# Hybrid retention and sliding-window layer: every SBUF place and PSUM bank named by the plan that orders the kernel

## The chip, the cores and the metric

The kernel runs on one core of one Trainium2 chip. The metric is the time of one execution in device microseconds (us); less is better. Below, PE is TensorE, PEld its weight loads, DVE is VectorE, ACT is ScalarE, POOL is GpSimd, and SP is the engine whose queue issues nearly all DMAs.

## The reference

One pre-normalised mixer layer over 2048 tokens of width 1024, all float32:

```python
h = rms_norm(x, norm_w)
proj = einsum('bsd,de->bse', h, w_in)                 # 1024 -> 2816
rq, rk, rv, rg, sq, sk, sv, sg = split(proj)
ro = retention(rotary(rq), rotary(rk), rv)            # 4 heads, chunks of 128, recurrent state
ro = group_norm(ro) * ret_norm_w * silu(rg)
so = sliding_window_attention(sq, sk, sv, ...)        # 8 query heads, 2 key heads, window 128,
so = so * silu(sg)                                    # QK-norm, relative bias, a sink per head
x = x + einsum('bse,ed->bsd', concat([ro, so]), w_out)
```

## The kernel before

The sequence is cut into 16 chunks of 128 tokens, handled as 8 pairs. The three wide parts of the input projection and the output projection are done as seven block products m for each pair p (a Strassen-like scheme: sums and differences of quarters of the weights and of x, then seven products instead of eight). Each float32 operand is split into a high and a low part (`hi`, on ACT; `lo`, on DVE), and each product is three matmuls (`acc<-w,x`), which make up most of PE's work. Beside them run the window attention (`attend`, `values`: tiles `lg`, `pm`, `pT`, `own`, `so`), the retention (`keys_of`, `update`, `retain`, `group_norm`: tiles `qk`, `state`, `sT`, `ro`), and the gates (`gate`: tiles `g`, `go`).

Tiles are turned (transposed) in one of two ways. Some go through PE. The others go by DMA: `turn_by_dma` has ACT pull the two 16-bit halves of the floats apart into a tile `apart`, stores that to DRAM (`planes_dram<-apart`), and loads it back with a transposing DMA. Other stores to DRAM that matter here are `g_dram<-c` (a gate that waits for its stage) and `ro_dram<-ro` (the normalised retention).

No engine's order is written by hand. Each piece of work is an `Op` with a cost by engine, a due time, and the buffers that it reads and writes. `Program.emit` is a planner: it keeps a clock for each engine, takes the op that can start first, calls its function, and so writes the program op by op. Class `Order` chains all instructions in that order, so the tile framework below it can't move any of them; the framework adds the semaphore waits.

The planner also keeps places. There are 93 SBUF tiles of 128x512 (tag "k"), 8 of 128x256 ("h"), 8 PSUM banks ("bank"), and a few places for each small tile. `slots[tag]` is the sorted list of the times at which, by the plan, the free places come free: the end of the last op that used one, plus `SEM` (0.06 us). An op that needs a place takes the first time of the list. The plan counts a DMA as ended 2.6 us after its turn on the bus (`dma`: `(0.15 + kb / 450, 2.6, issue)`).

Which physical place a tile gets is not the planner's decision. `alloc` asks a pool for a tile with `bufs=CAP[b.tag]`, and the framework hands out one of the free ones. In the built program that is, for the 128x512 tiles, the place whose last user stands first in the program's order, or one of the two next to it, in 1492 of 1502 reuses. When the last user of a place was a store, the new tile's first writer waits until that store has landed.

All instructions are recorded through one helper, so the profile puts almost everything on line 390; the tiles' names tell groups apart.

Of the kernel before, what the change touches and what calls it, by code (L numbers as in the profile page):

```python
# [29 lines left out]
F32 = mybir.dt.float32  # L30
# [9 lines left out]
P = 128  # L40
# [16 lines left out]
CAP = {"k": 93, "h": 8, "bank": 8}  # L57
SMALL, COUNTS = 3, {"ms": 1, "rxt": 1, "rqk0t": 1, "rqk1t": 1}
# [23 lines left out]
SEM = 0.06  # L82
# [19 lines left out]
def change(a, b):  # L102

    return 0.0 if a == b else LESSER if 0 < a < 3 and 0 < b < 3 else CHANGE
# [3 lines left out]
class Buf:  # L108


    def __init__(self, tag=None, shape=None, dtype=F32, name="", share=None, ap=None):
        self.tag, self.shape, self.dtype, self.name, self.share = tag, shape, dtype, name, share
        self.ap, self.left, self.end = ap, 0, 0.0
        self.writer, self.readers = None, []

    def __call__(self):
# [18 lines left out]
class Program:  # L135
# [33 lines left out]
    def emit(self):  # L169
        engines = self.engines  # L170
        avail = {e: [] for e in engines}
        free = dict.fromkeys(engines, 0.0)
        port, table, bus, cut = 0.0, None, 0.0, 0
        cap = dict(CAP)
        slots = {t: [0.0] * n for t, n in cap.items()}
        used = dict.fromkeys(SHARE, 0)
        count = len(self.ops)

        def offer(o):
            for e in o.cost:  # L180
                bisect.insort(avail[e], (o.due, o.n, o))

        for o in self.ops:
            if not o.left:
                offer(o)
        done, now = 0, 0.0
        while done < count:
            best = None
            for e, found in avail.items():
                top = None  # L190
                base = free[e]
                if e == "T" and not cut:
                    crowd = sum(o.set in CUTS and o.ready <= base for _, _, o in found[:48])
                for due, n, o in found[:48]:
                    if top is not None and top[0] <= base + 1e-9 and not e == "T":
                        break
                    occ, lat, shared = o.cost[e]
                    s = max(base, o.ready)
                    if e == "T" and o.set:
                        if cut and o.set in CUTS:  # L200
                            s = max(base, o.ready + INSIDE)
                            if change(cut, CUTS[o.set]) < CHANGE:
                                due -= SOONER
                        else:
                            s = max(base, o.ready + SETTLED)
                            if o.set in CUTS:
                                due += LATER - CROWD * min(crowd, MOST)
                    if shared and e != "Q":
                        s = max(s, port)
                    need, short, room = {}, False, 0.0  # L210
                    for b in o.new:
                        if b.ap is None:
                            need.setdefault(b.tag, []).append(b)
                    if any(due > now + AHEAD_OF.get(b.share, 1e9) for b in o.new):
                        continue
                    spare = 0
                    if e == "Q" and need:
                        if due > now + AHEAD:
                            break
                        spare = SPARE  # L220
                    for tag, bs in need.items():
                        if tag not in slots:
                            slots[tag] = [0.0] * COUNTS.get(tag, SMALL)
                        f = slots[tag]
                        if len(f) < len(bs) + (spare if tag == "k" else 0):
                            short = True
                            break
                        room = max(room, f[len(bs) - 1])
                        for share in {b.share for b in bs if b.share}:
                            many = used[share] + sum(b.share == share for b in bs)  # L230
                            if many > SHARE[share] - (spare if share in SPARED else 0):
                                short = True
                    if short:
                        continue
                    s, wait = max(s, room), 0.0
                    if e == "A" and o.set and table and o.set != table:
                        wait = 1.3
                        s += 2.0
                    if top is None or s < top[0] - 1e-9 or (s < top[0] + 1e-9 and due < top[1]):
                        top = (s, due, n, o, wait, room)  # L240
                if top is not None and (best is None or top[:3] < best[0][:3]):
                    best = top, e
            if best is None:
                self.stuck(avail, used, slots)
            (s, _, _, o, wait, room), e = best
            occ, lat, shared = o.cost[e]
            free_before = free[e]
            for e2 in o.cost:
                a = avail[e2]
                a.pop(bisect.bisect_left(a, (o.due, o.n)))  # L250
            for b in o.new:
                if b.ap is None:
                    slots[b.tag].pop(0)
                    if b.share:
                        used[b.share] += 1
                    b.ap = self.alloc(b)
            if e == "Q":
                occ, lat, more = o.cost[e]
                bus = max(bus, s) + occ
                free[e] = max(s + more, bus - BACKLOG)  # L260
                o.end = bus + lat
            else:
                if wait:
                    s = s - 2.0 + wait
                if e == "A" and o.set:
                    table = o.set
                free[e] = s + occ
                o.end = s + lat
                if shared:
                    port = s + occ  # L270
                if e == "T":
                    s = max(free_before, o.ready, room) if o.set else s
                    s += change(cut, CUTS.get(o.set, 0))
                    cut = ENDS.get(o.set, CUTS.get(o.set, 0))
                    free[e] = s + occ
                    o.end = s + lat
            o.seen = free[e]
            if e == "T" and o.set is None:
                now = max(now, o.due)
            o.go(engines[e])  # L280
            done += 1
            if LOG is not None:
                LOG.append((e, s, free[e], o))
            for b in o.bufs:
                b.left -= 1
                b.end = max(b.end, o.end)
                if not b.left and b.tag:
                    bisect.insort(slots[b.tag], b.end + SEM)
                    if b.share:
                        used[b.share] -= 1  # L290
            for d in o.after:
                d.left -= 1
                same = len(d.cost) == 1 and e in d.cost and e in ("T", "A", "Q") and not o.label.startswith("load")
                t = o.seen if same and e != "Q" else o.end + SEM
                if e == "Q" and now > 0:
                    t += LATE
                if t > d.ready:
                    d.ready, d.by = t, o
                if not d.left:
                    offer(d)  # L300
        self.time = max(free.values())
# [92 lines left out]
def layer(ctx, tc, xt, xfirst, xtok, nw, w_in, w_rn, qkw, sinks, biasg, rope, decays, dmask, gpow, w_out, out):  # L394
# [5 lines left out]
    sbuf = ctx.enter_context(tc.tile_pool(name="pool", bufs=1))  # L400
    little = ctx.enter_context(tc.tile_pool(name="small", bufs=SMALL))
    psum = ctx.enter_context(tc.tile_pool(name="psum", bufs=1, space=PSUM))
    dram = ctx.enter_context(tc.tile_pool(name="dram", bufs=1, space=DRAM))

    def alloc(b):
        if b.tag == "bank":
            return psum.tile([P, 512], F32, tag=b.tag, bufs=CAP[b.tag], name=b.name)
        if b.tag in ("k", "h"):
            n = 512 if b.tag == "k" else 256
            return sbuf.tile([P, n], b.dtype, tag=b.tag, bufs=CAP[b.tag], name=b.name)  # L410
        return little.tile(b.shape, F32, tag=b.tag, bufs=COUNTS.get(b.tag, SMALL), name=b.name)

    prog = Program(alloc, {"V": V, "G": G, "A": A, "Q": Q, "T": T})
    op = prog.op

# [1261 lines left out]
```

## Time and profile before

| | us |
|---|---|
| runs | 710.24, 712.25, 712.52 (median 712.25) |
| the profiled execution: its own time | 713.38 |
| its span | 711.6 |
| PE busy | 687.2 (97%) |
| DVE busy | 605.7 (85%) |
| ACT busy | 474.1 (67%) |
| DMA queue of SP, share of 16 engines | 84.4% |

The span runs from the first to the last instruction of the program; the profiled execution's own time is 1.8 us longer. A PE that is busy 97% of the span is still not at its peak: matmuls are pipelined, and while the granted clock is halved each of them takes twice as long and still counts as busy. In the views of waits a row reads: who waited, for whom, us in total, how many times, the longest. In the timeline a row reads: start, duration, engine, instruction, count, and in brackets the idle time ahead of it and what ended it.

### The profile page before, as it was taken

Reading aid. Unit: us, or ns where it says so; the run is one execution under the profiler, and the core shown is the slowest. Engines: PE = TensorE matmul, PEld = TensorE weight load, DVE = VectorE, ACT = ScalarE, POOL = GpSimd, SP = SyncE. Lnnn points to the kernel's source line nnn. Section 1 sums busy time; section 2 is a strip of 40 time slices with the busy share of each in tenths; the row PEclk is TensorE's granted clock in tenths of the full one; section 3 lists DMA queues with packets and bytes.
Section 4 is the critical chain, followed back from the end, with each engine's and each line's share of the span. In section 5 each row is a group of like instructions: output and inputs, shape, how many; then the busy total and the mean of one; then the engine's idle time right before and its main releaser. Section 6 shows DMA issues by size and latency. Waiting matters only on the chain. (4 is left out here: it accounts for less than half of the span.)

```text
span 711.6 us, 15589 instructions
## 1 busy us (share of the span) xinstructions
PE 687.2 (97%) x5428; PEld 580.3 (82%) x5428; DVE 605.7 (85%) x1483; ACT 474.1 (67%) x1122; POOL 42.7 (6%) x75
## 2 busy tenths in 40 slices
PE   9999999999999999999899799999989999999998
PEld 7888888889899999987687578888768787788886
DVE  6999877877998979999797779899788698999962
ACT  7666955666796576989577668896989844253300
POOL 1000000025120010101000000100000000000000
PEclk9999999999999999999999989999999999999999
DMA  9999945989988899999999899589799898314722
GB/s 326 385 343 311 386 163 181 358 278 279 311 218 222 185 318 312 317 283 281 305 236 285 207 240 287 128 258 289 200 333 313 195 273 261 119 44 159 275 107 97
DMA packets 171487, 179.07 MB, mean 252 GB/s; under 512 B 71824, under 2 KB 106768, under 8 KB 171408
## 3 DMA queue, kind: packets, MB, share of 16 engines
q1 hardware_dynamic: 171264, 178.07, 84.4%
q8 instruction: 43, 0.70, 0.4%
q14 instruction: 36, 0.29, 0.1%
q10 hardware_dynamic: 144, 0.00, 0.0%
HBM read 106.64 MB, written 56.69 MB: 230 GB/s over the span
## 5 line engine op out<-in xcount | busy, mean ns | idle before, releaser
L390 PE MATMUL acc<-w,x 128*128 128x512 f32 (+1 forms) x2700 | 598.9, 380 | 8.2 <-ACT s L390 3.8
L390 PEld LDWEIGHTS acc<-w,x 128*128 128x128 f32 x2700 | 495.8, 190 | 95.1 <-ACT s L390 5.1
L390 DVE TENSOR_TENSOR x<-x 128x512 fp32r<-128x512 f32 (+2 forms) x220 | 146.4, 686 | 20.3 <-ACT x L390 19.9
L390 ACT ACTIVATE x<-x 128x512 fp32r<-128x512 f32 (+1 forms) x187 | 111.4, 616 | 18.6 <-DVE x L390 12.7
L390 DVE TENSOR_TENSOR w<-w 128x512 fp32r<-128x512 f32 (+3 forms) x96 | 61.0, 655 | 4.6 <-ACT w L390 2.2
L390 ACT ACTIVATE pm<-lg,nm 128x128 f32<-128x128 f32 x128 | 49.7, 395 | 6.7 <-DMA planes_dram<-apart 3.4
L390 ACT ACTIVATE w<-w 128x512 fp32r<-128x512 f32 (+1 forms) x72 | 40.4, 602 | 18.1 <-DVE w L390 11.3
L390 DVE SCALAR_TENSOR_TENSOR w<-w,nw_sb 128x512 fp32r<-128x512 f32 (+3 forms) x72 | 49.0, 703 | 0.8 <-ACT w L390 0.7
L390 DVE TENSOR_TENSOR s<-acc,s 128x512 f32<-128x512 f32 (+1 forms) x64 | 41.6, 651 | 8.0 <-PE acc L390 7.9
L390 DVE CUSTOM_DVE_ANT_0 lg<-m,bias,nsnk 128x160 f32<-128x160 f32 x128 | 42.5, 379 | 6.5 <-PE m L390 6.3
L390 POOL TENSOR_SCALAR_AFFINE_SELECT own<-pT 64x512 f32<-64x512 f32 x32 | 25.6, 813 | 266.2 <-ACT pT L390 218.8
L390 DVE TENSOR_TENSOR t<-acc,t 128x512 f32<-128x512 f32 (+2 forms) x33 | 21.2, 641 | 18.8 <-PE acc L390 18.2
L390 ACT ACTIVATE x<-go 128x512 fp32r<-128x512 f32 x40 | 24.0, 624 | 14.3 <-PE acc L390 7.4
L390 ACT ACTIVATE s<-acc 128x512 f32<-128x512 f32 (+1 forms) x32 | 18.0, 563 | 18.7 <-PE acc L390 10.1
L390 DVE TENSOR_TENSOR x<-go,x 128x512 fp32r<-128x512 f32 x40 | 27.1, 683 | 3.4 <-ACT x L390 3.4
L390 ACT ACTIVATE w<-w,nw_sb 128x512 fp32r<-128x512 f32 (+3 forms) x44 | 28.1, 680 | 2.3 <-DMA w<-in_w_in 2.3
L390 ACT ACTIVATE apart<-qn 128x1024 uint16<-128x1024 uint16 x16 | 16.9, 1055 | 16.2 <-DVE qn L390 16.1
L390 ACT ACTIVATE ro<-ro,nmu,rg 128x128 f32<-128x128 f32 x64 | 25.1, 481 | 3.3 <-DVE nmu L390 3.3
L390 ACT ACTIVATE c<-acc 128x512 f32<-128x512 f32 (+1 forms) x24 | 13.4, 559 | 19.2 <-PE acc L390 16.5
L390 ACT ACTIVATION_READ_ACCUMULATOR pm<-lg,nm 128x1 f32 x128 | 24.8, 194 | 0.0
L390 DVE TENSOR_TENSOR t<-acc,s 128x512 f32<-128x512 f32 (+1 forms) x32 | 20.7, 648 | 4.2 <-PE acc L390 4.1
L390 ACT ACTIVATE xk<-xk 128x512 f32<-128x512 f32 x32 | 19.8, 620 | 5.5 <-DMA xk<-in_xtok 5.5
(133 smaller groups left out, 666.8 us busy)
## 6 DMA issues: line engine op xcount, KB each, us to landing
x<-in_xt SPq DMA_DIRECT2D x80, 256.0 KB, 5.2
x<-s_dram SPq DMA_DIRECT2D x64, 256.0 KB, 4.6
planes_dram<-apart SPq DMA_DIRECT2D x56, 256.0 KB, 4.8
w<-in_w_in SPq DMA_DIRECT2D x40, 256.0 KB, 4.8
s_dram<-x SPq DMA_DIRECT2D x32, 256.0 KB, 4.5
xk<-in_xtok SPq DMA_DIRECT2D x32, 256.0 KB, 5.3
res<-in_xtok SPq DMA_DIRECT2D x32, 256.0 KB, 5.0
w<-in_w_out SPq DMA_DIRECT2D x20, 256.0 KB, 5.6
```

Source lines behind the costliest of these rows:

```text
L390: return lambda *a, **k: self.order.put(op(*a, **k))
```

## The change

The planner's list of free places now holds pairs: the time at which a place comes free by the plan, and the number of the place. A buffer remembers the number that it was given, and gives it back with its end. `alloc` makes the number part of the tag and asks for one buffer of that tag. So each named place is a pool of one, and a tile goes to the place that the plan took: the one that by the plan came free first.

```diff
-        slots = {t: [0.0] * n for t, n in cap.items()}
+        slots = {t: [(0.0, i) for i in range(n)] for t, n in cap.items()}
...
-                        room = max(room, f[len(bs) - 1])
+                        room = max(room, f[len(bs) - 1][0])
...
-                    slots[b.tag].pop(0)
+                    b.place = slots[b.tag].pop(0)[1]
...
-                    bisect.insort(slots[b.tag], b.end + SEM)
+                    bisect.insort(slots[b.tag], (b.end + SEM, b.place))
...
     def alloc(b):
+        tag = f"{b.tag}{b.place}"
         if b.tag == "bank":
-            return psum.tile([P, 512], F32, tag=b.tag, bufs=CAP[b.tag], name=b.name)
+            return psum.tile([P, 512], F32, tag=tag, bufs=1, name=b.name)
         if b.tag in ("k", "h"):
             n = 512 if b.tag == "k" else 256
-            return sbuf.tile([P, n], b.dtype, tag=b.tag, bufs=CAP[b.tag], name=b.name)
-        return little.tile(b.shape, F32, tag=b.tag, bufs=COUNTS.get(b.tag, SMALL), name=b.name)
+            return sbuf.tile([P, n], b.dtype, tag=tag, bufs=1, name=b.name)
+        return little.tile(b.shape, F32, tag=tag, bufs=1, name=b.name)
```

No instruction moves: on every engine the rows of the built program stand in the same order, and the numbers of places are the same (93, 8, 8). What changes is the address of a tile, and with it the earlier user for whose end its first writer waits. Four places follow. Names in brackets are semaphores: DMAHW0 to DMAHW7 are raised by landing DMAs, the others by the engine of that name.

ACT, where the retention's outputs `ro` of one pair of chunks are copied from PSUM; before:

```order
L390 ACTIVATE qk_5978<-qk_5978,factors1_83 128x64 [waits DVE_49,PE_49]
L390 ACTIVATE qk_5978<-qk_5978,factors1_83 128x64 x3
L390 ACTIVATE ro_6051<-m_5929 128x2x128 [waits DVE_49,PE_49]
L390 ACTIVATE ro_6051<-m_5931 128x2x128 [waits PE_49]
L390 ACTIVATE ro_6077<-m_5930 128x2x128 [waits DMAHW4_49,Activation_49]
L390 ACTIVATE ro_6077<-m_5932 128x2x128 [waits PE_49]
```

The same place in the changed kernel:

```order
L390 ACTIVATE qk_5978<-qk_5978,factors1_83 128x64 [waits DMAHW1_49]
L390 ACTIVATE qk_5978<-qk_5978,factors1_83 128x64 x3
L390 ACTIVATE ro_6051<-m_5929 128x2x128 [waits DVE_49,PE_49]
L390 ACTIVATE ro_6051<-m_5931 128x2x128 [waits PE_49]
L390 ACTIVATE ro_6077<-m_5930 128x2x128
L390 ACTIVATE ro_6077<-m_5932 128x2x128 [waits PE_49]
```

The first writer of `ro_6077` waited for the store out of `apart_5989`, whose place it took over; now it waits for nothing.

ACT, at softmax weights `pm`, a split `x`, and a copy `s` of a product's bank; before:

```order
L390 ACTIVATE ro_5198<-m_5056 128x2x128 [waits PE_49]
L390 ACTIVATE pm_5164,den_5162<-lg_5139,nm_5132 128x128 [waits DMAHW4_49,DVE_49]
L390 ACTIVATE pm_5164,den_5162<-lg_5139,nm_5132 128x128
L390 ACTIVATE x_5221<-x_4897 128x512 [waits DMAHW7_49,DMAHW2_49,Activation_49]
L390 ACTIVATE s_5228<-acc_5118 128x512 [waits PE_49]
```

The same place in the changed kernel:

```order
L390 ACTIVATE ro_5198<-m_5056 128x2x128 [waits PE_49]
L390 ACTIVATE pm_5164,den_5162<-lg_5139,nm_5132 128x128 [waits DMAHW0_49,DVE_49]
L390 ACTIVATE pm_5164,den_5162<-lg_5139,nm_5132 128x128
L390 ACTIVATE x_5221<-x_4897 128x512 [waits DMAHW2_49]
L390 ACTIVATE s_5228<-acc_5118 128x512 [waits DMAHW4_49,PE_49]
```

The store of `apart` for which `pm_5164` waited (DMAHW4) is now waited for by `s_5228`, three instructions later; `pm_5164` waits for an older transfer, and `x_5221` no longer for the store of another `apart` (DMAHW7).

ACT, at a copy `c` and two `apart` in front of a copy `s`; before:

```order
L390 ACTIVATE qk_5539<-qk_5539,factors1_83 128x64 x4
L390 ACTIVATE c_5627<-acc_5441 128x512 [waits DMAHW2_49,PE_49,Activation_49]
L390 ACTIVATE apart_5633<-qk_5539 128x1024 [waits Activation_49]
L390 ACTIVATE apart_5648<-qn_5544 128x1024 [waits DVE_49]
L390 ACTIVATE s_5661<-acc_5612 128x512 [waits PE_49]
```

The same place in the changed kernel:

```order
L390 ACTIVATE qk_5539<-qk_5539,factors1_83 128x64 x3
L390 ACTIVATE c_5627<-acc_5441 128x512 [waits DVE_49,PE_49]
L390 ACTIVATE apart_5633<-qk_5539 128x1024 [waits DMAHW0_49,Activation_49]
L390 ACTIVATE apart_5648<-qn_5544 128x1024 [waits DMAHW2_49]
L390 ACTIVATE s_5661<-acc_5612 128x512 [waits PE_49]
```

The wait for the store `g_dram<-c` (DMAHW2) went from `c_5627` to `apart_5648`, two instructions later, and `apart_5633` got one for an earlier store.

SP, at the loads of the residual `res` in the output projection, before and then in the changed kernel:

```order
L390 DMA res_8752<-in_xtok 128x512 [waits DMAHW6_49]
L390 DMA res_8754<-in_xtok 128x512 [waits PE_49]
L390 DMA res_8778<-in_xtok 128x512 [waits DMAHW0_49,DVE_49,Activation_49]
L390 DMA res_8803<-in_xtok 128x512 [waits DMAHW1_49,PE_49,Activation_49]
L390 DMA res_9035<-in_xtok 128x512 [waits DMAHW2_49,DVE_49]
```

```order
L390 DMA res_8752<-in_xtok 128x512 [waits DVE_49,Activation_49]
L390 DMA res_8754<-in_xtok 128x512 [waits DMAHW2_49]
L390 DMA res_8778<-in_xtok 128x512 [waits DMAHW0_49,DVE_49]
L390 DMA res_8803<-in_xtok 128x512 [waits DMAHW1_49,PE_49]
L390 DMA res_9035<-in_xtok 128x512 [waits DVE_49]
```

Each load waits for the end of another tile than before; `res_8778` and `res_8803` now wait for an instruction of DVE and one of PE that stand later in the program than the ones before.

More of the change, by code (lines that the diff above doesn't have):

```diff
@@ L112, in __init__ @@
         self.tag, self.shape, self.dtype, self.name, self.share = tag, shape, dtype, name, share
-        self.ap, self.left, self.end = ap, 0, 0.0
+        self.ap, self.left, self.end, self.place = ap, 0, 0.0, None
         self.writer, self.readers = None, []
@@ L222, in emit @@
                         if tag not in slots:
-                            slots[tag] = [0.0] * COUNTS.get(tag, SMALL)
+                            slots[tag] = [(0.0, i) for i in range(COUNTS.get(tag, SMALL))]
                         f = slots[tag]
```

## The prediction

> **What bounds the kernel now.** First the head of the page: the span, and the busy time of the engines.
>
> ```profile
> span 711.6 us, 15589 instructions
> ...
> PE 687.2 (97%) x5428; PEld 580.3 (82%) x5428; DVE 605.7 (85%) x1483; ACT 474.1 (67%) x1122; POOL 42.7 (6%) x75
> ```
>
> PE is idle for 711.6 - 687.2 = 24.4 us, so that is nearly all that a change of waits can give back, beside time in which PE runs at a lower clock. Next the view of waits for PE (who waits, for whom, us in total, times, longest):
>
> ```profile
> PE m L390 <- ACT ro L390: 6.2, 2, 4.3
> PE acc L390 <- ACT s L390: 3.8, 3, 2.0
> PE m L390 <- DVE sT L390: 3.5, 2, 2.9
> ...
> PE acc L390 <- DVE w L390: 1.4, 1, 1.4
> ```
>
> PE never waits long for DMA. It waits for ACT and DVE. So the question is what these wait for ahead of a PE stall; ACT's own waits hold two large ones that end with a store, not with data that ACT reads:
>
> ```profile
> ACT s L390 <- DMA planes_dram<-apart: 7.2, 1, 7.2
> ...
> ACT ro L390 <- DMA planes_dram<-apart: 5.0, 1, 5.0
> ```
>
> Neither `s` nor `ro` reads `planes_dram`. These are waits for a place: the tile before it in the same place was still being stored. The timeline around the longest PE stall shows it:
>
> ```profile
> 400.78 1.06 ACT L390 ACTIVATE apart<-qk 128x1024 uint16<-128x1024 uint16 x1 [1.04 <-DMA ro_dram<-ro]
> ...
> 404.67 1.36 PE L390 MATMUL m<-v,qk 64*64 64x128 f32 x32 [1.84 <-ACT ro L390]
> ...
> 405.01 0.36 SPq L390 DMA_DIRECT2D planes_dram<-apart  x1
> ...
> 409.92 0.66 ACT L390 ACTIVATE ro<-m 128x256 f32<-128x256 f32 x2 [5.04 <-DMA planes_dram<-apart]
> ...
> 410.36 0.48 PE L390 MATMUL m<-ident,kn 128*128 128x128 f32 x1 [4.33 <-ACT ro L390]
> ```
>
> SP issues the store at 405.01, it lands 4.8 us later, ACT may then overwrite the place, and PE, which needs the bank that ACT empties, starts at 410.36. The stall has a second price. Two pieces of the chain of waits (start, duration, count), and rows of windows (window, length, busy us of PE, PEld, DVE, ACT and POOL, granted clock, DMA share, GB/s):
>
> ```profile
> 410.84 5.96 PE acc L390 x15
> ...
> 432.44 9.75 PE acc L390 x42
> ```
>
> ```profile
> 340.00:420.00 80.00, 69.53 (x703) 54.56 (x702) 62.76 (x192) 54.55 (x141) 2.39 (x4) 0.91 0.97 262
> 400.00:420.00 20.00, 13.83 (x135) 10.62 (x135) 12.07 (x42) 12.03 (x33) 0.95 (x2) 0.74 0.91 249
> 520.00:540.00 20.00, 17.10 (x155) 13.56 (x154) 17.48 (x44) 18.40 (x32) 0.00 (x0) 0.91 1.13 331
> 351.30:354.70 3.40, 3.40 (x10) 2.63 (x9) 3.40 (x8) 1.11 (x3) 0.00 (x0) 0.50 1.03 298
> 375.00:385.00 10.00, 8.54 (x39) 6.67 (x38) 7.67 (x25) 7.65 (x15) 0.00 (x0) 1.00 1.00 263
> ```
>
> Undisturbed, a matmul takes 9.75 / 42 = 0.232 us; behind the stall it takes 5.96 / 15 = 0.397 us, and the granted clock of 400 to 420 is 0.74. That is 5.96 - 15 x 0.232 = 2.5 us lost on top of the idle time. Outside the few stretches where the clock falls there is nothing else to gain from it.
>
> The end is set by PE: its last long run begins at 621.37, and whatever brings that point forward brings the end forward.
>
> ```profile
> 621.37 87.04 PE acc L390 x394
> ```
>
> **The change part by part.** No instruction is added, removed or moved; only the earlier user of each place, and so the wait of its next first writer, is another. Below, each wait of the changed program is read against this trace: it would have ended when its releaser ended here.
>
> C, 404 to 416. `ro_6077` waits for nothing any more, so ACT can run it right behind the copy at 404.5, and the 4.33 us in front of PE's 410.36 go. The `apart` at 400.78 waits for older stores of `ro`, which had landed by 397, so its 1.04 us go. The row of DVE ahead of that burst lost time to a place as well, and ACT's normalising of `ro` waited for it:
>
> ```profile
> 390.42 0.43 DVE L390 TENSOR_TENSOR qk<-tcos,tsin 128x256 f32<-128x256 f32 x1 [1.82 <-DMA g_dram<-c]
> ...
> 390.96 1.27 ACT L390 ACTIVATE ro<-ro,nmu,rg 128x128 f32<-128x128 f32 x3 [2.47 <-DVE nmu L390]
> ```
>
> That wait goes too. 1.04 + 1.82 is more than the 1.84 us of the stall at 404.67, so both of PE's waits for `ro` go: 6.2 us, and the slow matmuls behind them, 2.5: together 8.7.
>
> A, 350. The timeline:
>
> ```profile
> 347.26 0.40 ACT L390 ACTIVATE pm<-lg,nm 128x128 f32<-128x128 f32 x1 [1.81 <-DMA planes_dram<-apart]
> ...
> 349.25 0.63 ACT L390 ACTIVATE x<-x 128x512 fp32r<-128x512 f32 x1 [1.11 <-DMA planes_dram<-apart]
> 349.79 0.58 ACT L390 ACTIVATE s<-acc 128x512 f32<-128x512 f32 x1
> ...
> 350.42 4.85 PE L390 MATMUL acc<-w,x 128*128 128x512 f32 x13 [2.01 <-ACT s L390]
> ```
>
> `pm` and `x` lose their waits; `s` inherits the store that ended `pm`'s, at about 347.2, and so ends near 347.8 instead of 350.4. PE's 2.0 us go. The window at 351.3 shows the clock at 0.50: 4.85 - 13 x 0.232 = 1.8 us more. Together 3.8.
>
> B, 380:
>
> ```profile
> 372.71 0.41 SPq L390 DMA_DIRECT2D g_dram<-c  x1
> ...
> 377.36 0.60 ACT L390 ACTIVATE c<-acc 128x512 f32<-128x512 f32 x1 [2.05 <-PE acc L390]
> ...
> 379.75 0.59 ACT L390 ACTIVATE s<-acc 128x512 f32<-128x512 f32 x1
> ...
> 380.39 3.02 PE L390 MATMUL acc<-w,x 128*128 128x512 f32 x12 [1.46 <-ACT s L390]
> ```
>
> The view names PE for `c`'s wait, but the product that it copies was complete at 373.5; the other semaphore in its wait is that of the store issued at 372.71, some 4.5 us before. In the changed program `c` goes 2 us earlier and the second `apart` behind it takes over that wait, so `s` comes about 1.4 us earlier: 1.4.
>
> D, 590 to 601:
>
> ```profile
> 590.88 0.60 ACT L390 ACTIVATE s<-acc 128x512 f32<-128x512 f32 x1 [7.19 <-DMA planes_dram<-apart]
> ...
> 592.84 0.69 DVE L390 TENSOR_TENSOR w<-w 128x512 fp32r<-128x512 f32 x1 [1.47 <-DMA planes_dram<-apart]
> ...
> 600.93 1.43 PE L390 MATMUL acc<-w,x 128*128 128x512 f32 x5 [1.36 <-DVE w L390]
> ```
>
> ACT's `s` could start 2.3 us earlier, with its product. DVE's `w` then waits for the end of ACT's split and of the DVE instruction ahead, 1.3 us earlier, and the packed DVE row behind it follows. PE's waits of 0.35 (the third for `s`: 3.8 - 2.0 - 1.46) and 1.36 shrink by about 1.6 in all.
>
> A to D: 3.8 + 1.4 + 8.7 + 1.6 = 15.5. The stall of 2.9 us for `sT` near 528 stays: no wait for a place stands in front of it.
>
> What is late next. A to C ask for 13.9 us out of the 80 from 340 to 420. DVE is busy 62.76 of them and ACT 54.55, so both fit into 66. The DMA engines hardly do: a share of 0.97 over 80 us is 77.6, and the highest share of any stretch of 20 us is the 1.13 at 520. At that rate the same transfers need 77.6 / 1.13 = 68.7 us, so DMA caps the gain there at 11.3. Loads are issued well ahead, so this is a soft cap; I take it, because the stores on which places hang are among those transfers.
>
> New waits. The latest releasers, against this trace, are two loads of `res` on SP (2.5 us late at 612.4; a later matmul must end first) and a split of `x` on ACT, the third of this row, that must now let the first `w` of DVE end (1.2 us late):
>
> ```profile
> 612.42 0.33 SPq L390 DMA_DIRECT2D res<-in_xtok  x1
> ...
> 615.42 1.68 ACT L390 ACTIVATE x<-x 128x512 fp32r<-128x512 f32 x3 [1.42 <-DVE x L390]
> ...
> 617.02 1.89 DVE L390 TENSOR_TENSOR w<-w 128x512 fp32r<-128x512 f32 x3
> ...
> 625.44 1.89 DVE L390 TENSOR_TENSOR x<-x 128x512 fp32r<-128x512 f32 x3
> ...
> 635.17 3.38 SPq L390 DMA_DIRECT2D res<-in_xtok  x3
> ```
>
> SP issues nothing behind that load until 635.17, and DVE uses the split only with the second of its three rows from 625.44 on, so both are covered here at no cost. PE itself gets no wait that would have been late in this trace. Once PE is ahead, covers are thinner: I bound the new waits by 0 and 2.5 + 1.2 = 3.7, and with no row nearer to either end take 1.9.
>
> Sum: 11.3 + 1.6 - 1.9 = 11.0. The profiled execution, 713.4 us with 1.8 outside its span, would come to 702.4; it ran 1.1 above the median of 712.25, from which the forecast is 701.3.
>
> A rule weighs against one term. The Trainium skill, in "TensorE: Matmul & The Clock Gate", section "Part 1: The HAM clock gate", says that an idle window of about 3.4 us is what halves PE's clock. By that rule the 2.0 us stall at 350 would not, and the forecast without its 1.8 us would be 703.1; the trace differs, with a clock of 0.50 from 351.3 on, while after the 1.46 us stall at 380 it stayed at 1.00. The row decides.
>
> **The rivals.** *Everything returns* (faster still): DMA is no cap, because loads run ahead. For it: shares above 1 at 351 and 520. Against it, the DMA row of the page (tenths in 40 slices of 17.8 us), which is at 8 or 9 nearly throughout from slice 10 to 23, up to 427:
>
> ```profile
> DMA  9999945989988899999999899589799898314722
> ```
>
> 15.5 off the median gives 696.8; with part of the `sT` stall and its slow clock gone as well, about 694.
>
> *Only the bare waits return.* PE comes to the next input that is not ready soon behind each stall removed. For it: PE's waits are short and many engines are near full. The 4.3 of C, less some of the new waits, remain: 712.25 - 4.3 = 708, between 705 and 710.
>
> *No effect.* The waits for stores move to neighbours that PE waits for as well, as A's did to `s`. Against it: there the store lands 2.6 us before `s` ran. About 712.
>
> *Slower.* The mechanism is the clock: with transfers pressed together, stores land later than the 4.8 us seen, a place wait stalls PE for 2 us or more around 430 to 450, where the changed program has its other late waits (up to 1.1 us on SP, 0.9 on ACT), and each such stall costs its length plus about 2 us of half clock. It decides only if these stalls sum to more than 15.5 + 2.1, two stalls like C's; with two the time is about 712.25 - 15.5 + 2 x 8.7 = 714, more with a third.
>
> **How the numbers follow.** A change under 0.3% (2.1 us) can't be told from none. Chances: the forecast (gain 8 to 14) 0.42; everything returns 0.20; bare waits 0.24; no effect 0.08; slower 0.06. So faster 0.86, same 0.08, slower 0.06. The range takes in the forecast, the bare waits up to 709.5 and everything returned down to 694.5: 0.8 or a little more.
>
> **What would show it.** In the changed profile ACT should have no wait of several us that ends with a store; PE's two waits for `ro` should be gone, and the granted clock near 1.00 from 400 to 420; the 2.9 us for `sT` should be there; the last run of PE should start near 610 and still last 87 us. I am wrong if PE shows new stalls of 2 us or more with a lower clock between 420 and 600, or if the stalls go and PE then waits for loads.

## The result, and the profile after

The changed kernel took 703.36 us (median of five runs, 699.02 to 706.88) against 712.25 (710.24 to 713.59) beside it: a ratio of 0.988, 95% interval 0.983 to 0.993. Timed once more in another set, it took 705.30 against 710.24: 0.993, interval 0.990 to 0.995. Both are faster; the gain is 5 to 9 us. The kernel before itself spreads from 706.9 to 713.0 over 29 runs of one set, so single runs tell little here. One run of e9 below (752.47 us, at a granted clock of 0.85 where its other runs had 0.99) is a slow one and stands in no median.

The head of the page after, PE's and ACT's rows of the waits, and the last row of the chain of waits (start, duration, count):

```profile
span 701.6 us, 15585 instructions
...
PE 685.6 (98%) x5428; PEld 578.6 (82%) x5428; DVE 604.6 (86%) x1483; ACT 475.5 (68%) x1122; POOL 42.5 (6%) x75
```

```profile
PE m L390 <- ACT pT L390: 3.9, 2, 2.1
PE m L390 <- DVE sT L390: 3.3, 1, 3.3
...
ACT pT L390 <- DMA planes_dram<-apart: 4.8, 1, 4.8
...
ACT s L390 <- DMA so_dram<-so: 3.1, 1, 3.1
```

```profile
611.36 87.07 PE acc L390 x394
```

PE's two waits for `ro` (6.2 us) are gone, and so are those for `s` (3.8); those for `pT` grew from 0.8 us to 3.9. The last long run of PE starts 10.0 us earlier and lasts as long as before. ACT still waits for stores, at other places than before. The windows (window, length, busy us of PE, PEld, DVE, ACT and POOL, granted clock, DMA share, GB/s):

```profile
340.00:420.00 80.00, 75.23 (x867) 59.03 (x868) 69.21 (x212) 58.96 (x148) 3.07 (x4) 1.00 1.01 271
400.00:420.00 20.00, 17.59 (x225) 13.52 (x218) 14.69 (x52) 12.47 (x29) 1.45 (x2) 1.00 1.04 266
520.00:540.00 20.00, 20.00 (x111) 16.30 (x104) 17.18 (x51) 18.28 (x31) 0.00 (x0) 0.86 1.14 323
```

The clock from 400 to 420 went from 0.74 to 1.00, and in the same 80 us PE does 867 matmuls instead of 703. The two new stalls in the timeline after:

```profile
361.28 0.90 SPq L390 DMA_DIRECT2D so_dram<-so  x2
...
365.62 0.60 ACT L390 ACTIVATE s<-acc 128x512 f32<-128x512 f32 x1 [3.10 <-DMA so_dram<-so]
366.12 0.59 ACT L390 ACTIVATE pT<-m 128x512 f32<-128x512 f32 x1
...
366.76 0.66 PE L390 MATMUL m<-ident,pm 128*128 128x128 f32 x4 [1.76 <-ACT pT L390]
...
400.07 1.05 ACT L390 ACTIVATE apart<-qk 128x1024 uint16<-128x1024 uint16 x1
...
403.95 2.07 SPq L390 DMA_DIRECT2D a<-rq_dram  x2
406.13 0.84 SPq L390 DMA_DIRECT2D x<-s_dram  x2
407.06 0.38 SPq L390 DMA_DIRECT2D g<-g_dram  x1
407.53 0.38 SPq L390 DMA_DIRECT2D planes_dram<-apart  x1
...
412.85 0.60 ACT L390 ACTIVATE pT<-m 128x512 f32<-128x512 f32 x1 [4.78 <-DMA planes_dram<-apart]
...
413.50 1.09 PE L390 MATMUL m<-pT,vs 128*64 128x128 f32 x14 [2.15 <-ACT pT L390]
```

The `apart` that is full at 401.12 is stored only from 407.53 on, because SP's queue issues other DMAs ahead of it; the store lands at 412.77, and then `pT` may have its place. In the trace of before the same store lands at 416.01 and the same `pT` starts at 419.11: 3.1 us to spare. In the changed kernel ACT is free for `pT` at 408.07, 11 us earlier, and the store comes only 3.2 earlier. With `s` it is alike: in the trace of before `s` starts at 366.41, 0.55 us ahead of the landing at 366.96 of the store for which it waits in the changed kernel, and here it waits 3.1.

What this costs is seen in PE's lead, the start of a matmul in the trace of before less the start of the same matmul in the other trace: for the matmul of `ident,kn` behind the second wait for `ro` it is 410.36 - 400.62 = 9.7 us. The table has how much the lead grew or shrank over each stretch, in us, at the times of the trace of before, for one profiled execution of each kernel (described below). Left out are the stretches up to 340 (-4.3 in all in e1, -1.4 to 1.7 in the others) and from 379 to 402 (0.0 to 0.2).

| stretch (step) | after | again | e2 | e3 | e4 | e11 | e6 | e8 | e9 | e1 | e5 | e6 again |
|---|---|---|---|---|---|---|---|---|---|---|---|---|
| 340-355 (A) | 4.8 | 2.3 | 3.7 | -0.8 | 3.1 | 5.3 | 5.3 | 4.8 | 5.3 | 3.0 | 3.9 | 5.3 |
| 355-372 | -2.9 | -3.5 | -2.9 | 0.0 | -6.3 | -0.4 | -0.6 | -0.4 | 0.0 | -1.2 | -0.4 | -2.0 |
| 372-379 (B) | 1.6 | 1.6 | 1.6 | 1.4 | 1.6 | 1.6 | 1.6 | 0.2 | -0.2 | 1.6 | -1.0 | 1.6 |
| 402-417 (C) | 9.2 | 8.9 | 8.7 | 4.2 | 8.5 | 8.0 | 9.2 | 9.2 | 9.2 | 0.0 | 8.9 | 9.2 |
| 417-460 | -4.0 | -4.6 | -4.4 | -1.4 | -4.5 | -3.2 | -4.3 | -2.7 | -5.5 | 0.0 | -4.6 | -3.2 |
| 460-590 | -0.4 | -0.3 | -1.7 | -0.7 | -1.9 | -3.0 | -0.7 | 0.0 | -1.5 | 0.6 | -2.4 | -1.2 |
| 590-621 (D) | 2.0 | 2.0 | 2.0 | 1.6 | 1.8 | 1.8 | 2.0 | 2.0 | 1.9 | 2.0 | 2.0 | 2.0 |

In the first column 17.6 us come from A to D, and 7.3 are lost again, 6.9 of them in the two stretches of the stalls shown.

Not all of the 17.6 need be the change's. In e1 the 128x512 tiles have the places of before, and it gains 2.0 at D all the same; e3, which exchanges places for C alone, gains 1.6 there. The store behind the stall at D took 7.9 us to land in the profiled execution of before (issued at 582.87, landed at 590.80) and 6.1 in e1, where it was over before `s` had its product. The timeline of e1:

```profile
588.61 0.60 ACT L390 ACTIVATE s<-acc 128x512 f32<-128x512 f32 x1 [4.80 <-PE acc L390]
```

So D is not shown to come from the places. C is: it is 0.0 in e1. At A and B, e1 comes late by 4.3 and 2.5 us and makes up there what PE of before spent waiting.

### The profile page after: what moved, and what is told of

The parts are those of the page before. It is cut to its first block, busy times and chain, and to the rows that moved or that the text cites. A ratio compares the mean times of both kernels' runs of the same rounds, so it can differ in the third digit from the quotient of the medians.

```text
span 701.6 us, 15585 instructions
## 1 busy us (share of the span) xinstructions
PE 685.6 (98%) x5428; PEld 578.6 (82%) x5428; DVE 604.6 (86%) x1483; ACT 475.5 (68%) x1122; POOL 42.5 (6%) x75
## 4 chain that ended last, share of the span: by engine, by line
PE 75%; DVE 14%; DMA 6%; ACT 2%; issue 2%; SPq 0%; DVEq 0%; ACTq 0%
PE acc L390 64%; PE m L390 10%; DVE x L390 4%; DVE w L390 2%; DVE lg L390 2%; DVE go L390 2%; DMA g<-g_dram 2%; ACT ro L390 1%; DVE t L390 1%; DMA planes_dram<-apart 1%; DVE s L390 1%; DMA w<-in_w_out 1%; DMA x<-s_dram 1%; DMA vd<-aq_dram 1%; DMA so_dram<-so 1%
## 5 line engine op out<-in xcount | busy, mean ns | idle before, releaser
L390 DVE TENSOR_TENSOR x<-x 128x512 fp32r<-128x512 f32 (+2 forms) x220 | 148.0, 695 | 17.3 <-ACT x L390 17.0
L390 ACT ACTIVATE w<-w 128x512 fp32r<-128x512 f32 (+1 forms) x72 | 41.0, 603 | 20.2 <-DVE w L390 11.3
L390 PE MATMUL m<-ks,qT 64*32 64x160 f32 x1024 | 23.2, 300 | 0.6 <-issue 0.6
```

The costliest lines, as they stand in the source:

```text
L390: return lambda *a, **k: self.order.put(op(*a, **k))
```

## The experiments

The theory at the start: the gain is the time that ACT and DVE no longer wait for stores to leave a place, and the time is that of before less the stalls removed plus the new ones. Rivals: addresses, banks or the naming itself; everything from C; the DMA cap of the prediction. In the last column, the us (and number) of waits of ACT and DVE for a store, added up over the rows of the view of waits whose releaser writes to `..._dram` or `out`; for before 27.3 + 4.6 = 31.9 in 16 + 3, of ACT and of DVE.

| kernel | ratio to before, 95% interval | median us | waits for stores |
|---|---|---|---|
| before | | 709.3 to 712.3 by set | 31.9 (19) |
| after, first time | 0.988 (0.983 to 0.993) | 703.36 | 16.3 (13) |
| after, again | 0.993 (0.990 to 0.995) | 705.30 | 24.0 (16) |
| e1: banks alone | 1.001 (0.999 to 1.003) | 711.07 | 28.4 (19) |
| e2: mirrored addresses | 0.993 (0.991 to 0.996) | 705.52 | 23.7 (14) |
| e3: C alone | 0.998 (0.996 to 1.000) | 708.43 | 24.6 (21) |
| e4: A to D alone | 0.997 (0.995 to 1.000) | 709.18 | 28.5 (17) |
| e11: e4 and five more | 0.995 (0.992 to 0.997) | 705.84 | 19.6 (12) |
| e5: after, two stalls removed | 0.990 (0.987 to 0.993) | 702.56 | 13.9 (12) |
| e6: stores counted at 4.8 us | 0.989 (0.987 to 0.991) | 701.60 | 8.5 (4) |
| e6 again | 0.989 (0.986 to 0.992) | 702.14 | 6.8 (4) |
| e8: by measured ends | 0.992 (0.989 to 0.994) | 704.63 | 6.8 (5) |
| e9: e6 and three exchanges | 0.991 (0.988 to 0.995) | 703.80 | 3.3 (3) |
| e7: first in program order | 1.025 (1.022 to 1.027) | 726.17 | 64.0 (25) |

**Addresses, banks, names.** e1 names banks and small tiles by the plan, and leaves the large tiles to the pool:

```diff
-            return sbuf.tile([P, n], b.dtype, tag=tag, bufs=1, name=b.name)
+            return sbuf.tile([P, n], b.dtype, tag=b.tag, bufs=CAP[b.tag], name=b.name)
```

> PSUM banks and small tiles are named by the plan as in the changed kernel; the 128x512 and 128x256 tiles come from the pool as before, so every instruction waits for the same releasers as before. Theory of the waits (the gain is the time that ACT and DVE no longer wait for stores to leave a place): no change, 712 us, ratio 1.00 within 0.3%, with PE's two waits for ro (6.2 us) still there. Rival, that the banks or the naming itself bring the gain: about 703 us, ratio 0.988.

The time did not change, and the first row of PE's waits is that of before within 0.1:

```profile
PE m L390 <- ACT ro L390: 6.1, 2, 4.2
```

e2 turns the addresses of the changed kernel round:

```diff
+    for i in reversed(range(CAP["bank"])):
+        psum.tile([P, 512], F32, tag=f"bank{i}", bufs=1, name="first")
+    for t, n in (("k", 512), ("h", 256)):
+        for i in reversed(range(CAP[t])):
+            sbuf.tile([P, n], F32, tag=f"{t}{i}", bufs=1, name="first")
```

> The changed kernel with its addresses turned round: the first of the 93 places stands where the last stood, and so for the 8 half tiles and the 8 banks. Every tile keeps its place number, so every wait is that of the changed kernel; only addresses and banks are others. Theory of the waits: 703 us again (ratio 0.988), with the same two new stalls of PE behind pT and s near 413 and 366 and the same wait for sT. Rival, that it is which addresses or banks work side by side: another time, toward 712 us or beyond 1% away from 703.

The changed kernel itself was timed in the next set:

> The changed kernel itself once more, beside the others of this set: ratio to before between 0.988 (its first timing) and 0.993 (the same waits at mirrored addresses). Both theories of the rest expect the same here.

0.993 both times, and the same stall behind `pT` in the timeline of e2:

```profile
413.82 0.60 ACT L390 ACTIVATE pT<-m 128x512 f32<-128x512 f32 x1 [4.13 <-DMA planes_dram<-apart]
...
414.47 1.09 PE L390 MATMUL m<-pT,vs 128*64 128x128 f32 x14 [1.48 <-ACT pT L390]
```

So neither addresses nor banks make the gain. That naming is not it either, e7 shows: named places, but the free one whose last user stands first in the program.

```diff
-                    b.place = slots[b.tag].pop(0)[1]
+                    slots[b.tag].pop(0)
+                    b.place = places[b.tag].pop(0)[1]
...
-                    bisect.insort(slots[b.tag], (b.end + SEM, b.place))
+                    bisect.insort(slots[b.tag], b.end + SEM)
+                    bisect.insort(places[b.tag], (done, b.place))
```

> Named places as in the changed kernel, but of the free ones the op takes that whose last user stands first in the program; the order is untouched. Read against the trace of before, 79 places released by a store were free for less than 2 us when taken over (60 before, 26 changed), and 56 for less than 0.3 (25 and 6). Theory of the slack: slower than before, ratio 1.005 to 1.02, with waits of ACT and DVE for stores of over 30 us in all. Rival, that naming a place by itself brings the gain: 0.988 to 0.993.

It is slower by 2.5%, more than expected. The largest stall of its timeline is of the kind of the change, doubled:

```profile
427.32 0.37 SPq L394 DMA_DIRECT2D planes_dram<-apart  x1
...
430.66 0.60 ACT L394 ACTIVATE pT<-m 128x512 f32<-128x512 f32 x1 [9.63 <-DMA planes_dram<-apart]
...
431.31 0.91 PE L394 MATMUL m<-pT,vs 128*64 128x128 f32 x6 [6.17 <-ACT pT L394]
```

With the same order of instructions, the choice among free places alone moves the time from 0.989 to 1.025. In the large it goes with the waits for stores (64.0 us in e7, 31.9 before, 6.8 to 24.0 in the changed kernel and e6), but not in the small: e4 has 28.5 us of them at 0.997, e11 19.6 at 0.995, and the changed kernel in its second timing 24.0 at 0.993.

**The steps alone.** e3 writes the places that the 128x512 tiles have in the kernel before out as a table and exchanges two places from a given tile on, three times; banks and small tiles are named as in e1. (Where the pool lent a place between a tile's allocation and its first write, the table can't, and takes another.)

```diff
+            if b.tag == "k":
+                return sbuf.tile([P, n], b.dtype, tag=f"k{next(places)}", bufs=1, name=b.name)
...
-    62, 12, 35, 63, 4, 66, 27, 36, 41, 0, 13, 49, 1, 75, 44, 64, 86, 71, 52, 50, 5, 39, 20, 29, 0,
+    62, 12, 35, 63, 4, 66, 27, 36, 41, 0, 13, 49, 1, 75, 44, 64, 86, 71, 50, 52, 5, 39, 20, 29, 0,
```

That is the first of its exchanges, of places 52 and 50.

> The kernel before with its own places written out as a table, and three exchanges of two places each, so that qk at 390, apart at 401 and ro at 410 follow tiles that are long gone (step C alone). Theory of the waits: C's whole gross gain as the trace of the changed kernel has it, 9.2 us, since the new late waits of the changed kernel at 366 and 413 are not among these places: 703 us, ratio 0.987. By the prediction's own term for C, 8.7: 703.5. Rival, that PE runs into the next late input behind a removed stall: only the bare waits, 6.2 or less, 706 to 709.

```profile
403.43 1.15 ACT L458 ACTIVATE x<-x 128x512 fp32r<-128x512 f32 x2 [4.09 <-DMA ro_dram<-ro]
...
405.85 1.89 PE L458 MATMUL m<-v,qk 64*64 64x128 f32 x32 [3.12 <-ACT ro L458]
```

This is the timeline of e3 (the table shifts its lines, so the helper is line 458). The three waits are gone, and ACT stops at another one among them: the split `x` takes the place of an older `ro`, and it starts at 403.43, when that store has landed. In the trace of before ACT came to it after that. C brought 4.2 us instead of 9.2, and 0.2% of the time.

e4 makes the exchanges of A, B and D as well; the first of them, in the same table:

```diff
-    86, 72, 32, 29, 40, 80, 37, 11, 23, 77, 69, 51, 62, 31, 58, 86, 85, 28, 91, 84, 72, 65, 70, 15,
+    86, 72, 32, 29, 85, 80, 37, 11, 23, 77, 69, 70, 62, 31, 58, 86, 40, 28, 91, 84, 72, 65, 51, 15,
```

> As the kernel with step C alone, with five more exchanges: pm at 347 and x at 349 (A), c at 377 (B), s and w at 591 to 593 (D). No other wait moves by more than 0.33 us against the trace of before. Theory of the waits: the gains of A to D as the changed kernel's trace has them, 4.8 + 1.6 + 9.2 + 2.0 = 17.6 us, without its new late waits: 695 us, ratio 0.975, or 697 by the prediction's terms (15.5). Rival, the DMA cap of the prediction: A to C bring 11.3 at most, D 1.6: 699 to 700, with a DMA share of at most 1.13 from 340 to 400. Rival, that stalls removed come back downstream as new waits whatever the places: about 703, as the changed kernel.

All three estimates missed: 0.997. The third had the right mechanism, though with too small a loss: by the table of leads A to D came (15.0), and 12.7 were lost, 6.3 of them from 355 to 372, behind the one wait that was 0.33 us late by the trace of before. The timeline of e4:

```profile
356.05 0.38 SPq L458 DMA_DIRECT2D g_dram<-c  x1
...
360.87 0.60 ACT L458 ACTIVATE s<-acc 128x512 f32<-128x512 f32 x1 [5.82 <-DMA g_dram<-c]
...
362.95 0.52 PE L458 MATMUL m<-ks,qT 64*32 64x160 f32 x8 [3.05 <-ACT so L458]
```

ACT comes earlier, the store does not: it is issued at 356.05 instead of 355.76 and lands at 360.76 instead of 358.16. The theory that stalls add up fell here; the second one was that what is lost goes into the next places freed just in time, and that places with more slack keep the gain. e11 gives five of those in e4's trace another place, the first of them so:

```diff
-    57, 80, 41, 12, 10, 23, 80, 51, 52, 59, 20, 92, 53, 35, 90, 54, 26, 9, 18, 25, 52, 33, 19, 55,
+    57, 80, 41, 12, 10, 23, 53, 51, 52, 59, 20, 92, 80, 35, 90, 54, 26, 9, 18, 25, 52, 33, 19, 55,
```

> The kernel with the exchanges of A to D, and five more, at the places where its own trace shows ACT or DVE held by a store at the next reuse: s at 361, apart at 411, x at 420, w at 432, tcos at 434. PE lost 6.0 us from 355 to 365 and 3.9 from 425 to 440 there. Theory of the slack (these waits ate the gain of A to D): about 10 us come back, ratio to before 0.983, 698 us. Rival, that PE's other inputs are late anyway (nothing to do with places): no more than 3 us, 0.993 or above.

0.995: by the ratios about 2 of the 10 us came back, which is the rival's size. In the profiled execution, which ran faster than the median, the two stretches lost 3.6 instead of 10.8, and what is left of the loss from 417 to 460 stands behind a load (below).

**Slack everywhere.** e6 keeps the plan and its order, but counts a place as free 2.2 us later where a DMA was its last user.

```diff
+STORE = 2.2
...
+                b.real = max(b.real, o.end + (STORE if e == "Q" else 0.0))
...
+                    bisect.insort(places[b.tag], (b.real, b.place))
```

> The changed kernel, but a place that a DMA was the last to use counts as free 2.2 us later than the plan had it, 4.8 us after its turn, which is how long these stores took in the trace; the order of the program is untouched. Read against the trace of before, places released by a store that were free for less than 2 us when taken over: 60 before, 26 in the changed kernel, 7 here. Theory of the slack (what was lost of the gain went into places freed just in time, which a faster ACT or DVE meets too early): 6 to 8 us below the changed kernel, ratio to before about 0.982. Rival, the DMA cap: nothing more than the changed kernel has, 0.988 to 0.993.

> The kernel whose plan counts a store as landed after 4.8 us, once more beside the others of this set: 0.987 to 0.991 as at its first timing.

e8 takes all places from such a table, made with the ends that the trace of the changed kernel shows; 1390 of its 1595 entries differ from that kernel's, here the first line that does:

```diff
-    74, 75, 76, 77, 78, 79, 80, 81, 82, 83, 84, 85, 86, 87, 88, 89, 90, 91, 92, 4, 6, 14, 15, 9, 11,
+    74, 75, 76, 77, 78, 79, 80, 81, 82, 83, 84, 85, 86, 87, 88, 89, 90, 91, 92, 4, 14, 6, 15, 9, 20,
```

> The order as always; places from a table that takes, at each allocation, the free place whose last user ended first by the trace of the changed kernel. Read against that trace, 2 places released by a store were free for less than 0.3 us when taken over (18 in the changed kernel by its own places), against the trace of before 13 for less than 2 us (26 in the changed kernel). Theory of the slack: 5 to 8 us below the changed kernel, ratio to before about 0.982, and no wait of ACT for a store of over 1.5 us between 340 and 600. Rival, the DMA cap: 0.988 to 0.993.

e5 is the changed kernel with two exchanges (24 entries), and e9 is e6 with three (31), both with the 128x256 tiles from the pool again; the first of each:

```diff
-    20, 33, 47, 48, 29, 5, 68, 59, 34, 25, 84, 47, 37, 51, 44, 46, 29, 39, 40, 86, 12, 58, 77, 47,
+    20, 33, 47, 48, 29, 5, 68, 59, 37, 25, 84, 47, 34, 51, 44, 46, 29, 39, 40, 86, 12, 58, 77, 47,
```

```diff
-    61, 14, 79, 26, 35, 75, 18, 57, 84, 58, 76, 14, 9, 19, 23, 28, 40, 55, 59, 83, 71, 38, 88, 27,
+    61, 14, 79, 26, 35, 75, 18, 57, 84, 58, 76, 83, 9, 19, 23, 28, 40, 55, 59, 14, 71, 38, 88, 27,
```

> The changed kernel's own places as a table, with two exchanges: s at 366 and pT at 413 follow tiles that are long gone. In front of these two PE lost 3.0 and 4.0 us of its lead. Theory of the slack: up to 7 us below the changed kernel, 0.981 to 0.983, less what the next tight place takes. Rival as above: within 0.3% of the changed kernel, 0.988 to 0.993.

> The kernel whose plan counts a store as landed after 4.8 us, its places as a table, with three exchanges at its last waits for stores in that part: apart at 355 and 403, tsin at 413. In its trace tsin waited 3.83 us for a store, PE then 2.60 for nm, and PE's lead fell by 4.3 us from 417 to 440. Theory of the slack: about 4 us below that kernel, ratio to before 0.983. Rival: the lead is lost there anyway, 0.989.

All of them lie at 0.989 to 0.992, which is what the rivals gave: the DMA cap for e6 and e8, a lead lost anyway for e5 and e9. With the waits for stores down from 16 or 24 us to 3, the ratio stays within 0.4% of either timing of the changed kernel, and these intervals overlap with its own. Against its second timing e6 is 3.7 us lower in the median of the same set; e9, with still fewer waits, is 1.7 above e6 in the set that they share. The second theory expected a large gain of more slack, and that is wrong. What stands where the lead is lost in e6 is one more store; in e9, where that wait was taken away, it is a load. The timelines of e6 and of e9:

```profile
413.05 0.69 DVE L396 TENSOR_TENSOR tsin<-a,phases 128x512 f32<-128x512 f32 x1 [3.83 <-DMA planes_dram<-apart]
...
417.31 0.99 PE L396 MATMUL m<-state,qkT 64*64 64x128 f32 x27 [2.60 <-DVE nm L396]
```

```profile
423.20 0.32 SPq L458 DMA_DIRECT2D g<-g_dram  x1
...
427.29 0.72 ACT L458 ACTIVATE g<-g,rstd_all 128x512 f32<-128x512 f32 x1 [1.79 <-DMA g<-g_dram]
...
428.55 1.28 ACT L458 ACT_TABLE_LOAD   x1
...
430.49 0.71 PE L458 MATMUL m<-ident,pm 128*128 128x128 f32 x2 [0.51 <-ACT pm L458]
...
432.03 1.49 PE L458 MATMUL m<-ident,pm 128*128 128x128 f32 x6 [0.83 <-ACT pm L458]
```

Behind those two stalls the clock of e9 falls as well (window, length, busy us, granted clock, DMA share, GB/s, as above), which is part of its 5.5 us:

```profile
433.44:436.85 3.41, 3.41 (x10) 2.64 (x9) 1.92 (x8) 2.72 (x10) 1.47 (x2) 0.50 1.08 378
```

The same load holds ACT in the timeline of e11, and PE waits longer behind it:

```profile
421.13 0.38 SPq L458 DMA_DIRECT2D g<-g_dram  x1
...
425.69 0.73 ACT L458 ACTIVATE g<-g,rstd_all 128x512 f32<-128x512 f32 x1 [3.92 <-DMA g<-g_dram]
...
428.90 0.71 PE L458 MATMUL m<-ident,pm 128*128 128x128 f32 x2 [1.05 <-ACT pm L458]
```

In e8 it is 2.9 us at 426.7. So from 417 to 460 the kernels of the table that gain 8 us or more at C give back 2.7 to 5.5 us: by their timelines behind a store where one holds a place, and behind this load in e8, e9 and e11. Both go through SP's queue. Behind the load ACT has hardly a pause (it is busy 9.0 of the 10 us from 426 to 436 in e8), and the stall of 0.8 us for a later `pm` is the same in e8, e9 and e11, however late the load; so ACT's own work is a rival. Neither an earlier issue nor less work on ACT was tried, so that the load is the cause of the rest is argued and not shown.

## Why the prediction was right, and where it was not

*The direction and its cause* were right. Waits for places that a store had yet to leave were what PE's stalls at C hung on, and e1, e2 and e7 leave no room for addresses, banks or naming.

*C* was forecast at 8.7 and measured at 9.2 and 8.9, with the clock at 1.00 from 400 to 420. *B*, 1.4, was 1.6 both times. *D*, 1.6, was 2.0, but e1 has the same 2.0 with the places of before: the step took the stall for a cost of the places, and it is not shown to be one. *A*, 3.8, was 4.8 and 2.3: in the second profile `s`, which inherited the store, was still held by it, and PE behind `s`, as the timeline of the second profile shows:

```profile
349.83 0.60 ACT L390 ACTIVATE s<-acc 128x512 f32<-128x512 f32 x1 [2.43 <-DMA planes_dram<-apart]
...
350.48 1.88 PE L390 MATMUL acc<-w,x 128*128 128x512 f32 x7 [1.00 <-ACT s L390]
```

The sum of 15.5 was 17.6 and 14.8, and without D 15.6 and 12.8.

*The DMA cap* of 11.3 for A to C did not act as argued. At 417 the leads gained since 340 are 12.8 in the changed kernel and 15.6 in e6, with a share of 1.01 in the row of 340 to 420 above and 1.03 in e6. Where e6 loses the lead again, the share is lower still:

```profile
420.00:440.00 20.00, 19.87 (x122) 15.84 (x124) 17.81 (x62) 16.12 (x48) 1.48 (x2) 1.00 0.85 262
```

At the two new stalls it is the order and delay of single DMAs in SP's queue that counts, not the rate of all. The working has a slip here too. It says that without A's 1.8 us of slow clock the forecast would be 703.1; but A to C would then still ask for 12.1, more than the cap of 11.3, and the forecast would have stayed at 701.3.

*The new waits* are the term that failed: 1.9 forecast, bounds 0 to 3.7, and 6.9 and 8.1 measured from 355 to 372 and 417 to 460. The step read each new wait against the trace of before and kept the ones late there. It should have asked how much slack the others had: of some 175 reuses of a place that a store leaves, 26 had under 2 us there, while A to C bring PE, and ACT with it, forward by 4 to 12 us, and the stores do not come forward as much. The two errors, a cap that wasn't and waits too small, cancelled in part: 13.9 - 11.3 + 1.9 = 4.5 us taken off, where some 7 to 8 were lost. That the sum came near all the same owes something to luck: two wrong terms lay on opposite sides.

*The `sT` stall* stayed, as said (3.3 us), and its slow clock got longer: 0.86 from 520 to 540 instead of 0.91. "ACT should have no wait of several us that ends with a store" was wrong: 4.8 for `pT`, 3.1 for `s`. New stalls of 1.8 and 2.2 us came, at 366 and 413 rather than 430 to 450, but without a lower clock, so the slower rival found no ground.

*The rival of the bare waits*, 708 us, deserves its due. Its mechanism, that PE soon comes to the next input that is not ready, is what took about half of the gain, though at C the slow clock was won back with the stall. By ratio the forecast was 701.3 / 712.25 = 0.985 and this rival 0.994; the two timings, 0.988 and 0.993, lie between them. *Everything returns* (696.8, 0.978) is excluded for this change, and no other choice of places tried came below 0.989, even with 3 us of waits for stores left.

## What to carry to other kernels

When a place in a pool is reused, look at how its last user ends: a store ends long after the engine that filled the tile is done, and a planner that counts it too short, or a pool that takes places in program order, hands out places that are not free; among the same 93 places and in the same order that choice was worth 3.6% between the worst and the best kernel here. A removed stall is worth its time only as far as the next tight point behind it, so read the slack of the later reuses and loads, not only whether they were late. The stalls removed in one trace summed to 15 to 18 us here; 5 to 9 came. And see whether a stall stands in a second execution too: one of about 2 us, D, stood in one trace of the kernel before and not in that of e1, which has the same places.

## What the runs showed of the hardware

The delay of the store behind `pT` was mostly ahead of its issue. In the changed kernel the `apart` above was full at 401.12, its store issued at 407.53 and landed at 412.77: 6.4 us in SP's queue and 5.2 from there on, where the plan counts 2.6 after its turn. From 401.90 to 407.53 SP issued the nine DMAs that stood ahead of it, one in 0.63 us on average. In the trace of before, with ACT later, the same store was issued at 411.82, as soon as its `apart` was full (411.80).

The length of a stall alone does not tell whether the clock falls. In e1 a stall of 1.97 us was followed by a clock of 0.50; in e6 the one of 2.60 at 417.31 was not. The timeline of e1, and windows of e1, of e6, of before (around the stalls of 2.0 us at 350 and 1.46 at 380) and of the changed kernel:

```profile
329.56 1.23 PE L390 MATMUL acc<-w,x 128*128 128x512 f32 x3 [1.97 <-ACT x L390]
```

```profile
328.18:331.59 3.41, 1.78 (x6) 0.85 (x6) 2.84 (x14) 3.41 (x16) 0.00 (x0) 1.00 0.86 255
331.59:335.00 3.41, 3.38 (x11) 2.80 (x12) 2.02 (x6) 2.86 (x10) 0.76 (x1) 0.50 1.13 302
```

```profile
412.85:416.26 3.41, 1.87 (x9) 1.11 (x7) 3.21 (x8) 0.55 (x1) 0.00 (x0) 1.00 1.23 193
416.26:419.67 3.41, 2.36 (x95) 2.07 (x96) 3.41 (x21) 2.96 (x6) 0.00 (x0) 1.00 1.12 351
```

```profile
347.89:351.30 3.41, 1.40 (x7) 0.83 (x6) 1.50 (x5) 2.30 (x6) 0.00 (x0) 1.00 1.05 187
378.61:382.02 3.41, 1.95 (x9) 1.37 (x8) 1.14 (x4) 3.41 (x7) 0.00 (x0) 1.00 1.03 267
```

```profile
518.70:525.50 6.80, 5.93 (x42) 4.71 (x43) 6.18 (x17) 6.80 (x14) 0.00 (x0) 0.50 1.12 304
```

Up to the end of PE's work, the slow stretches of the fourteen traces are 3.41 us long, or two or three times that: 6.83 in the changed kernel from 518.70, 10.24 in before from 405.92. Within a trace they begin whole multiples of 3.413 us apart: in before at 351.30, 405.92 and 528.80, which is 16 and 36 times. So the traces show where the windows lie, and the rows above are cut on them. What counts is PE's idle time inside one window. Of the windows at full clock in the fourteen traces, the 26 in which PE was idle for 1.7 us or more were all followed by one at 0.50; of the 2751 with less than 1.4, none was; of the 16 between, 5 were. Of the windows already at 0.50, the nine with 0.6 us or more of idle time were followed by another such window, and the 31 with less than 0.4 by full clock; so the stretch of before from 405.92 came to be three windows long. The window of before that ends at 351.30 has 3.41 - 1.40 = 2.01 us, and the clock falls; the one with the stall at 380 has 1.46, and it stays. The stall of e6 is cut by a window's edge at 416.26, which leaves 1.54 us on the one side and 1.05 on the other. PE's ends are modelled in the profile, so the bound is rough.

The Trainium skill, in "TensorE: Matmul & The Clock Gate", section "Part 1: The HAM clock gate", says that activity is judged in windows of about 3.4 us that run freely, whatever the kernel does; the lengths and the starts agree with that. Its figure of a whole idle window disagrees with these traces, where about half a window, 1.4 to 1.7 us, is enough.

At the granted clock of 0.50 the matmuls of the products start 0.43 us apart (before, 351.6 to 354.2), against 0.23 undisturbed: 1.8 times as long.
